# A decoder layer on one core: dense quarters taken by the slab, gated sums turned a step later, a reciprocal moved

## The chip, the cores and the metric

The kernel runs on one core of a Trainium2 chip. The time is the device time of one execution, in microseconds (us). The core has four compute engines with queues of their own: TensorE (PE in the rows; PEld is its weight load), VectorE (DVE), ScalarE (ACT) and GpSimd (POOL). SyncE (SP) issues the large weight loads. Engines wait for each other through semaphores.

## The reference, cut to what matters

One decoder layer, 256 tokens, width 2048, all in float32.

```python
mod = silu(c) @ w_ada + b_ada                       # six vectors: shift, scale, gate, twice
h = rmsnorm(x) * (1 + sc_a) + sh_a
mixed = sigmoid(g_a) * (out_a @ w_proj_a) + sigmoid(g_b) * (hm @ w_proj_b)   # attention, mLSTM
x = x + gt_a * (mixed @ w_out)
t = rmsnorm(x) * (1 + sc_m) + sh_m
# router: one of 4 groups, then 2 of its 8 experts for each token, softmax weights -> comb
hg, hu = t @ w_gate_e, t @ w_up_e                   # 32 experts, each 2048 x 512
out = sum over experts of (silu(hg) * hu * comb) @ w_down_e                  # each 512 x 2048
x = x + gt_m * out
```

An expert's weights are 12 MB: 8 slabs of 1 MB for gate and up, 4 for down.

## The kernel before, in words

The first half of the program is the mixer: projections of the normed input (`half_pair`, `wide_gemm`), attention and mLSTM, all with each weight split into two float32r halves (`split`, L202 on ScalarE and L203 on VectorE). A half slab of weights is pushed, split, and multiplied one push later; after each push `tick` runs one step of the generators that wait in the list `side` and, now and then, one product of the adaLN matrix (`ada`, L156, on VectorE).

The mixer's end: `gate(i)` and `proj(i)` (L900 on) run over column blocks of 512. For blocks 4 to 7, `proj` multiplies the product by the gate (L905), adds the other mixer's part (L907), and calls `turn_over`, which transposes the sum with eight PE transposes (tile `mt`) and splits it into `mxh` and `mxl`. Then the output projection (`wo`) runs over 16 blocks of 128 columns; beside it `scaled` and `logit` (L1018 on) build the scaled residual `xg`, the router's logits `lb` and the shift's part `sh`. Expert 0 is a static dense expert: its 12 slabs are loaded during the output projection.

The router (L1066 on): the reciprocal norm as a column (`rcol`) and as a broadcast tile (`rstd2`, L1074), then group choice, expert choice and a ranking of the experts by their number of tokens, mostly tiny VectorE operations. Expert numbers reach SyncE through register loads (L1245, L1252). `tiles` turns the residual back to rows beside it.

The experts: `first` is expert 0, dense, over all 256 tokens and a shift column; a second dense one (`HEAVY`) is the expert ranked first. The others go in stacks of four (once two) experts (`LIGHT`), each with 32 (64) gathered tokens, so that four matmuls share the array. `prep` gathers a stack's tokens: masks `G` on VectorE, transposes `cb`, 64 matmuls `xb`. A light step uses one slab of each of its experts; a stack has 8 gate-up steps (tile `gu<-ring,xg`), then `silu` and the next stack's `prep`, then 4 down steps (`yb`, then `ob` back to tokens). A dense slab is used in four quarters, each four matmuls, with a `yield 0.25` after each (`gu<-xg,raw` for the first dense expert, `gu<-xg,ring` and `dd<-at,ring` for the second).

What sets the order: SyncE follows program order (`manual_schedule`). PE follows it too while `in_order` is set, which it is from the first light step until the dense stream ends; elsewhere a planner orders PE, VectorE and ScalarE. The loop at L1430 on merges the two streams: it takes the next piece from the dense stream (`i` = 0) unless that one is ahead by its share (`done[i] / total[i]`, with a dense share `HEAVY_SHARE` of 0.2; pieces of the second dense expert count twice). After an `"act"` piece the other stream is forced `SKIP[i]` times. Before the loop, `BEFORE` quarters of the first dense expert are put in the program.

Loads go through `ring` (`next_slot`, L1091 on): slots are taken from the front and put back at the end, so they serve in turn. The ring starts with four slots (three `w8`, one `v8`); `freed` adds one for each slab of the first dense expert that is used up, except slabs 0 and 7, until it has 14. A slot that is new in the ring is a fresh tile (load at L1104), which takes over the space of an earlier tile of its pool. A slot in use again is loaded at L1106. SyncE waits there until the matmuls of the slot's last slab are done, and all later loads stand behind.

Of the kernel before, what the change touches and what calls it, by code (L numbers as in the profile page):

```python
# [13 lines left out]
AF = mybir.ActivationFunctionType  # L14
# [4 lines left out]
P = 128  # L19
T = 256  # L20
D = 2048
KT = D // P
# [8 lines left out]
SKIP = [1, 2]  # L31
BIG2 = 3
FOR_XG = (0, 7)
EARLY = (1, 1)
BEFORE = 6
FIRST = "prrrtrtrtrtr"
HEAVY_SHARE = 0.2
W4 = 3
# [30 lines left out]
def decoder_layer_kernel(ctx, tc, xT, c, pos, cols_d, const_d, mask_d, w_ada, w_head, w_half, w_blk, w_mlv, w_pa, w_pb, w_out,  # L69
                         w_uq, w_ukv, w_rt, w_gu, w_dn, outT):  # L70
    nc = tc.nc
    act, vec, pool = nc.scalar, nc.vector, nc.gpsimd
# [20 lines left out]
    def bank(name):  # L93
        return psum.tile([P, 512], F32, name=name, tag="bank")
# [15 lines left out]
    def by2(x):  # L110
        return x.rearrange("p (a t) -> p a t", t=T)
# [4 lines left out]
    mod = keep.tile([P, 96], F32, name="mod")  # L116
# [3 lines left out]
    ones = keep.tile([P, P], F32, name="ones")  # L120
    rstd2 = keep.tile([P, T], F32, name="rstd2")
    warm = keep.tile([P, 1], F32, name="warm")
    rcol = keep.tile([P, 2], F32, name="rcol")
    brow = keep.tile([P, 36], F32, name="brow")
    lg = keep.tile([P, 2, 40], F32, name="lg")

    def col(name, i=0, n=1, p0=0, p1=P):
        s = COLS[name].start + i
        return cols[p0:p1, s:s + n]
# [64 lines left out]
    def pair(name, dt=F32):  # L194
        return by2(t2(name, dt))
# [12 lines left out]
    def split_act(src, name, make=None):  # L208
        hi, lo = [make(name + x, "tx" + x, F32R) if make else pair(name + x, F32R) for x in "hl"]
        act.activation(hi, src, AF.Copy)  # L210
        vec.tensor_tensor(lo, src, hi.bitcast(F32), op=ALU.subtract)
        return hi, lo
# [27 lines left out]
    side, pend = [], []  # L240
    ticks, headless = [0], [False, 0]

    def step():
        while side:
            try:
                next(side[0])
                return
            except StopIteration:
                side.pop(0)
# [546 lines left out]
    def pick(lst, i):  # L796
        return lambda k: lst[k // 2][i][:, k % 2]
# [88 lines left out]
        wide_gemm([w_blk[i, g] for g in range(4)], "ga", hhk, hlk, after)  # L886

    def turn_over(nh):
        for j in range(2):
            b = bank("mt")  # L890
            for i in range(2):
                for tt in range(2):
                    o = i * T + tt * P
                    pe.transpose(b[:, o:o + P], gated[nh][tt][:, (2 * j + i) * P:(2 * j + i + 1) * P], ident)
            mxs[2 * nh + j] = split_act(by2(b), "mx")

    def proj(i):
        nh = i % 4
        src, w = (oT, w_pa) if i < 4 else (hm, w_pb)

        def after(bs):
            store = mixed if i < 4 else gated
            for tt in range(2):
                t = store[nh][tt]
                vec.tensor_tensor(t, bs[tt], t, op=ALU.mult)  # L905
                if i >= 4:
                    vec.tensor_tensor(t, t, mixed[nh][tt], op=ALU.add)  # L907
            if i >= 4:
                turn_over(nh)

        if nh == 0:
            while src[3] is None:
                step()
        wide_gemm([w[nh, g] for g in range(2)], "pjb", pick(src, 0), pick(src, 1), after)
# [76 lines left out]
    wr = a1.tile([P, KT * 36], F32, name="wr")  # L991
    nc.scalar.dma_start(wr, w_rt)
    accs = t2("accs")
    lb, sh = bank("lb"), bank("sh")
# [20 lines left out]
    def logit(n, xg):  # L1015
        yield
        w = wr[:, n * 36:(n + 1) * 36]
        for tt in range(2):  # L1018
            pe.matmul(lb[:, tt * 36:(tt + 1) * 36], xg[:, tt * P:(tt + 1) * P], w, start=n + tt == 0, stop=False)
        for m in ((0, 1) if n == 0 else (n + 1,) if n < KT - 1 else ()):  # L1020
            pe.matmul(sh[:, 0:36], mod[:, 48 + m:49 + m].to_broadcast([P, P]), wr[:, m * 36:(m + 1) * 36], start=m == 0,
                      stop=m == KT - 1)
        if n == KT - 2:
            vec.tensor_tensor(brow, sh[:, 0:36], col("route_b", 0, 36), op=ALU.add)

    for n in range(KT):
# [23 lines left out]
    through = [0]  # L1050
# [20 lines left out]
    pe.matmul(sb2[:, :T], ones, accs[:, :T], start=True, stop=False)  # L1071
    pe.matmul(sb2[:, :T], ones, last[0][:, :T], start=False, stop=True)
    act.activation(rstd2, sb2[:, :T], AF.Sqrt, bias=epsc, scale=1.0 / D)
    vec.reciprocal(rstd2, rstd2)  # L1074
    for _ in range(EARLY[1]):
        next(first)
    phase_a.close()
# [320 lines left out]
    for _ in (*route, *tiles):  # L1398
        pass
    pinned.clear()  # L1400

    def unit(u):
        if u[0] == "dense":
            r = u[1]
            return dense(lambda: expert(r), lambda: R["perm"][:, r:r + 1].to_broadcast([32, P]), lambda: R["qT"][:, 1], xgs)
        return stack(u[1], u[2], u is LIGHT[-1])
# [18 lines left out]
    n_heavy = HEAVY_SHARE * n_light  # L1425
    for _ in range(BEFORE):
        next(first)
    pre[LIGHT[0][1]] = prep(*LIGHT[0][1:])
    in_order.append(1)
    streams, total, done = [heavy, light], (n_heavy, n_light), [0.0, 0.0]  # L1430
    forced = []
    while any(streams):
        i = forced.pop(0) if forced else int(done[0] / total[0] > done[1] / total[1])
        if not streams[i]:
            i = 1 - i
        got = next(streams[i], None)
        if got == "act":
            forced = [1 - i] * SKIP[i]
        elif got:
            done[i] += got * (2 if i == 0 and through[0] == 12 else 1)  # L1440
        else:
            streams[i] = None
        if not streams[0]:
            in_order.clear()
# [164 lines left out]
```

## Time and profile before

| What | Value |
|---|---|
| median of 3 runs (lowest to highest) | 1629.94 us (1629.08 to 1633.8) |
| the profiled execution's own time | 1629.09 us |
| its span on the profile | 1627.2 us |
| PE busy | 1382.4 us, 85% |
| VectorE busy | 750.0 us, 46% |
| ScalarE busy | 441.7 us, 27% |
| DMA moved | 560.70 MB, mean 345 GB/s |

The page gives busy time over the whole span, so it mixes stages with different limits. The slices (its second part) cut the span into 40 equal pieces and show the stages apart. The chain follows the last instruction back, at each step to what released it. A window row gives the busy time of each engine within one stretch, the granted TensorE clock (1.00 is 2.4 GHz) and the rate of the DMA.

### The profile page before, as it was taken

How to read it: one execution, taken by the hardware profiler on the slowest of the kernel's cores; microseconds unless marked ns; L12 is line 12 of the kernel's file. 1: busy time of each engine (PE TensorE's matmuls, PEld its weight loads, DVE VectorE, ACT ScalarE, POOL GpSimd, SP SyncE). 2: the span in 40 equal slices, each digit the busy share in tenths (PEclk: the TensorE clock that was granted, in tenths of full speed). 3: DMA queues.
4: the chain of work that ended last, by engine and by line, in shares of the span. 5: the costliest groups of instructions: out<-in, count | busy, mean ns of one | idle time of the engine just before them, and what ended most of it. 6: DMA issues, size and time to landing. Idle time of an engine off the chain costs nothing.

```text
span 1627.2 us, 21430 instructions
## 1 busy us (share of the span) xinstructions
PE 1382.4 (85%) x8290; PEld 960.9 (59%) x8290; DVE 750.0 (46%) x1113; ACT 441.7 (27%) x646; POOL 83.8 (5%) x91
## 2 busy tenths in 40 slices
PE   7899999999999999999978997867889756656766
PEld 5698998878877777899844753533445313213212
DVE  5878699879777778975401220210222301201202
ACT  3134765445754464333200100100100001001000
POOL 0150014000000000022000000000000000000000
PEclk9899999999999999999999997988999978888899
DMA  9978767888677788886498999899999699999997
GB/s 369 395 276 334 275 222 284 315 288 301 259 263 262 256 351 341 306 327 246 165 376 372 387 421 421 365 394 421 421 416 420 286 421 421 420 420 421 420 421 302
DMA packets 78877, 560.70 MB, mean 345 GB/s; under 512 B 8753, under 2 KB 9009, under 8 KB 12721
## 3 DMA queue, kind: packets, MB, share of 16 engines
q1 hardware_dynamic: 78482, 558.84, 86.4%
q8 instruction: 67, 1.10, 0.3%
q10 hardware_dynamic: 288, 0.44, 0.1%
q14 instruction: 40, 0.33, 0.1%
HBM read 569.73 MB, written 2.10 MB: 351 GB/s over the span
## 4 chain that ended last, share of the span: by engine, by line
PE 45%; DMA 33%; DVE 10%; issue 5%; ACT 3%; SPq 1%; POOL 0%; ACTq 0%; DVEq 0%; POOLq 0%
DMA ring<-in_w_gu_dram 24%; DMA ring<-in_w_dn_dram 8%; PE gu L78 7%; PE hp L78 6%; PE wo L78 5%; PE ga L78 5%; DVE raw L156 4%; PE pjb L78 3%; PE yb L78 3%; DVE whl L203 3%; PE dd L78 2%; PE xb L78 2%; PE vb L78 2%; PE hb L78 2%; SPq L1106 1%
## 5 line engine op out<-in xcount | busy, mean ns | idle before, releaser
L78 PE MATMUL gu<-ring,xg 128*32 128x512 f32 (+1 forms) x1664 | 259.1, 721 | 132.2 <-DMA ring<-in_w_gu_dram 132.1
L203 DVE TENSOR_TENSOR whl<-raw,whl 128x1024 fp32r<-128x1024 f32 (+1 forms) x210 | 253.2, 1216 | 82.0 <-ACT whl L202 81.1
L202 ACT ACTIVATE whl<-raw 128x1024 fp32r<-128x1024 f32 (+1 forms) x210 | 216.9, 1037 | 256.4 <-PE ga L78 61.4
L78 PEld LDWEIGHTS gu<-ring,xg 128*32 128x32 f32 (+1 forms) x1664 | 64.0, 130 | 305.8 <-DMA ring<-in_w_gu_dram 157.4
L156 DVE SCALAR_TENSOR_TENSOR raw<-raw,cond 128x2048 f32<-128x2048 f32 x96 | 220.7, 2300 | 16.5 <-DMA raw<-in_w_ada_dram 16.4
L78 PE MATMUL ga<-whl,hh 128*128 128x512 f32 x512 | 169.5, 401 | 1.3 <-DVE whl L203 1.3
L78 PE MATMUL yb<-ring,aT 128*32 128x512 f32 (+1 forms) x832 | 117.4, 655 | 56.5 <-DMA ring<-in_w_dn_dram 52.8
L78 PE MATMUL hp<-hh,whl 128*128 128x256 f32 x640 | 120.9, 288 | 3.4 <-DVE whl L203 3.2
L1332 DVE SCALAR_TENSOR_TENSOR s<-gu,wc,s 128x512 f32<-128x512 f32 x7 | 5.2, 750 | 231.2 <-PE gu L78 231.2
L78 PEld LDWEIGHTS ga<-whl,hh 128*128 128x128 f32 x512 | 96.0, 188 | 25.4 <-issue 3.1
L1259 DVE SCALAR_TENSOR_TENSOR xs<-ob,mod,xs 128x256 f32<-128x256 f32 x112 | 46.5, 477 | 136.4 <-PE ob L78 136.4
L1331 ACT ACTIVATE s<-gu 128x512 f32<-128x512 f32 x7 | 4.2, 596 | 384.2 <-PE gu L78 384.2
L78 PEld LDWEIGHTS yb<-ring,aT 128*32 128x32 f32 (+1 forms) x832 | 30.7, 120 | 127.0 <-issue 92.1
L78 PEld LDWEIGHTS hp<-hh,whl 128*128 128x128 f32 x640 | 101.9, 194 | 5.8 <-DVE whl L203 4.2
L78 PE MATMUL ga<-whl,hl 128*128 128x512 f32 x256 | 99.9, 390 | 0.0
L78 PE MATMUL wo<-mxh,whl 128*128 128x256 f32 x512 | 96.8, 286 | 0.2 <-DVE whl L203 0.2
L78 PE MATMUL hp<-hl,whl 128*128 128x256 f32 x320 | 91.2, 285 | 0.0
L78 PEld LDWEIGHTS wo<-mxh,whl 128*128 128x128 f32 x512 | 80.9, 191 | 0.4 <-DVE whl L203 0.4
L78 PE MATMUL wo<-mxl,whl 128*128 128x256 f32 x256 | 72.4, 283 | 0.0
L1344 ACT ACTIVATE yh<-yb 128x512 fp32r<-128x512 f32 (+1 forms) x29 | 16.9, 583 | 199.2 <-PE yb L78 198.7
L1279 DVE TENSOR_REDUCE wc<-cb 128x1 f32<-128x256 f32 x7 | 3.0, 424 | 137.9 <-PE cb L83 137.9
L78 PEld LDWEIGHTS hp<-hl,whl 128*128 128x128 f32 x320 | 62.1, 194 | 0.6 <-issue 0.5
(370 smaller groups left out, 2014.7 us busy)
## 6 DMA issues: line engine op xcount, KB each, us to landing
ring<-in_w_gu_dram SPq DMA_DIRECT2D x216, 1024.0 KB, 15.5
ring<-in_w_dn_dram SPq DMA_DIRECT2D x104, 1024.0 KB, 18.8
raw<-in_w_ada_dram SPq DMA_DIRECT2D x96, 1024.0 KB, 6.8
raw<-in_w_blk_dram SPq DMA_DIRECT2D x32, 1024.0 KB, 6.2
raw<-in_w_half_dram SPq DMA_DIRECT2D x20, 1024.0 KB, 5.0
raw<-in_w_out_dram SPq DMA_DIRECT2D x16, 1024.0 KB, 5.1
raw<-in_w_head_dram SPq DMA_DIRECT2D x16, 704.0 KB, 7.2
raw<-in_w_mlv_dram SPq DMA_DIRECT2D x8, 1024.0 KB, 4.8
```

The costliest lines, as they stand in the source:

```text
L78: ins = nc.tensor.matmul(*args, **kw)
L156: vec.scalar_tensor_tensor(raw, raw, 1.0, cond, op0=ALU.mult, op1=ALU.mult, accum_out=mod[:, i:i + 1])
L202: keep(act.activation(hi, raw, AF.Copy))
L203: keep(vec.tensor_tensor(lo, raw, hi.bitcast(F32), op=ALU.subtract))
L1106: nc.sync.dma_start(slot[:, s], src[:, s], cond=cond())
L1259: vec.scalar_tensor_tensor(xs[:, d], src, mod[:, 80 + d:81 + d], xs[:, d], op0=ALU.mult, op1=ALU.add)
L1279: vec.tensor_reduce(wc, cb[:, :T], axis=AX.X, op=ALU.add)
L1331: act.activation(s, gu[0], AF.Silu)
L1332: vec.scalar_tensor_tensor(s, gu[1], wc, s, op0=ALU.mult, op1=ALU.mult)
L1344: act.activation(yh[:, s], yb[:, s], AF.Copy)
```

## The change

The stream takes a whole slab (four quarters) of the second dense expert at once, and after a light stack's `"act"` the dense stream is forced once instead of twice while that expert runs. Two quarters fewer of the first dense expert are put ahead of the streams. `turn_over` becomes a generator in `side`: for the first three column blocks its transposes come one step after the sums, and its two halves come in two steps. In the router the shift's products use a one-column operand and give one row; ScalarE copies the row, and one matmul with ones spreads it over the partitions. The reciprocal of `rstd2` moves from the router's start to behind the router and the row tiles, kept in program order there.

```diff
--- before.py
+++ after.py
@@ -32,7 +32,7 @@
 BIG2 = 3
 FOR_XG = (0, 7)
 EARLY = (1, 1)
-BEFORE = 6
+BEFORE = 4
 FIRST = "prrrtrtrtrtr"
 HEAVY_SHARE = 0.2
 W4 = 3
@@ -886,6 +886,8 @@
         wide_gemm([w_blk[i, g] for g in range(4)], "ga", hhk, hlk, after)
 
     def turn_over(nh):
+        if nh < 3:
+            yield
         for j in range(2):
             b = bank("mt")
             for i in range(2):
@@ -893,6 +895,7 @@
                     o = i * T + tt * P
                     pe.transpose(b[:, o:o + P], gated[nh][tt][:, (2 * j + i) * P:(2 * j + i + 1) * P], ident)
             mxs[2 * nh + j] = split_act(by2(b), "mx")
+            yield
 
     def proj(i):
         nh = i % 4
@@ -906,7 +909,7 @@
                 if i >= 4:
                     vec.tensor_tensor(t, t, mixed[nh][tt], op=ALU.add)
             if i >= 4:
-                turn_over(nh)
+                side.append(turn_over(nh))
 
         if nh == 0:
             while src[3] is None:
@@ -1018,9 +1021,10 @@
         for tt in range(2):
             pe.matmul(lb[:, tt * 36:(tt + 1) * 36], xg[:, tt * P:(tt + 1) * P], w, start=n + tt == 0, stop=False)
         for m in ((0, 1) if n == 0 else (n + 1,) if n < KT - 1 else ()):
-            pe.matmul(sh[:, 0:36], mod[:, 48 + m:49 + m].to_broadcast([P, P]), wr[:, m * 36:(m + 1) * 36], start=m == 0,
-                      stop=m == KT - 1)
+            pe.matmul(sh[0:1, 0:36], mod[:, 48 + m:49 + m], wr[:, m * 36:(m + 1) * 36], start=m == 0, stop=m == KT - 1)
         if n == KT - 2:
+            act.activation(brow[0:1], sh[0:1, 0:36], AF.Copy)
+            pe.matmul(sh[:, 0:36], ones[0:1], brow[0:1], start=True, stop=True)
             vec.tensor_tensor(brow, sh[:, 0:36], col("route_b", 0, 36), op=ALU.add)
 
     for n in range(KT):
@@ -1071,7 +1075,6 @@
     pe.matmul(sb2[:, :T], ones, accs[:, :T], start=True, stop=False)
     pe.matmul(sb2[:, :T], ones, last[0][:, :T], start=False, stop=True)
     act.activation(rstd2, sb2[:, :T], AF.Sqrt, bias=epsc, scale=1.0 / D)
-    vec.reciprocal(rstd2, rstd2)
     for _ in range(EARLY[1]):
         next(first)
     phase_a.close()
@@ -1398,6 +1401,7 @@
     for _ in (*route, *tiles):
         pass
     pinned.clear()
+    tc.keep_in_program_order(vec.reciprocal(rstd2, rstd2))
 
     def unit(u):
         if u[0] == "dense":
@@ -1433,9 +1437,12 @@
         i = forced.pop(0) if forced else int(done[0] / total[0] > done[1] / total[1])
         if not streams[i]:
             i = 1 - i
+        whole = i == 0 and through[0] == 12
         got = next(streams[i], None)
+        if whole and got not in (None, "act"):
+            got += sum(next(streams[0]) for _ in range(3))
         if got == "act":
-            forced = [1 - i] * SKIP[i]
+            forced = [1 - i] * (1 if through[0] == 12 else SKIP[i])
         elif got:
             done[i] += got * (2 if i == 0 and through[0] == 12 else 1)
         else:
```

## Rows read from the trace of the kernel before

**Rows 1.** the page's slices (40 of 40.7 us each): GB/s that the DMA moved in each

```profile
GB/s 369 395 276 334 275 222 284 315 288 301 259 263 262 256 351 341 306 327 246 165 376 372 387 421 421 365 394 421 421 416 420 286 421 421 420 420 421 420 421 302
```

**Rows 2.** windows: from:to length, busy us (xcount) of each engine, clock, DMA share, GB/s

```profile
1050.00:1060.00 10.00, 8.16 (x57) 5.03 (x56) 3.85 (x10) 2.30 (x8) 0.00 (x0) 1.00 0.37 126
...
1280.00:1290.00 10.00, 9.96 (x69) 5.04 (x66) 4.43 (x10) 0.60 (x1) 0.00 (x0) 1.00 0.06 26
...
1290.00:1300.00 10.00, 1.89 (x8) 1.33 (x8) 2.94 (x10) 0.00 (x0) 0.00 (x0) 0.83 0.70 274
```

**Rows 3.** the chain that ended last, expert stretch: start us, us, engine, tile, line

```profile
1056.80 1.75 PE gu L78 x8
...
1058.56 0.33 SPq L1106
...
1166.80 7.15 PE xb L78 x64
...
1289.96 1.94 PE dd L78 x8
...
1291.92 0.34 SPq L1106
```

**Rows 4.** one tile's view, ring, 780 to 1310: time from issue to landing

```profile
DMA to landing us min/median/max: 4.8/13.9/20.8
```

**Rows 5.** PE's timeline, light gate-up step 1: start us, us, operation, [idle before]

```profile
819.40 4.95 PE L78 MATMUL gu<-ring,xg 128*32 128x512 f32 x32 [5.69 <-DMA ring<-in_w_gu_dram]
```

**Rows 6.** PE's timeline, light step 7, gather's transposes, down step 0

```profile
883.91 3.64 PE L78 MATMUL gu<-ring,xg 128*32 128x512 f32 x32 [0.97 <-DMA ring<-in_w_gu_dram]
...
893.05 0.30 PE L83 MATMUL cb<-const,G 128*128 128x128 f32 x1 [2.95 <-DVE G L1271]
...
909.68 3.64 PE L78 MATMUL yb<-ring,aT 128*32 128x512 f32 x32 [0.69 <-ACT aT L1338]
```

**Rows 7.** windows, end of the first dense expert

```profile
880.00:890.00 10.00, 9.03 (x56) 4.90 (x54) 1.40 (x4) 0.69 (x4) 0.00 (x0) 1.00 0.55 217
...
910.00:920.00 10.00, 10.00 (x72) 5.73 (x68) 2.43 (x5) 0.60 (x1) 0.00 (x0) 1.00 0.73 278
```

**Rows 8.** SyncE's timeline, the same stretch

```profile
887.62 0.33 SPq L1104 DMA_DIRECT2D ring<-in_w_dn_dram  x1
```

**Rows 9.** PE's timeline, first transposes of three column blocks

```profile
624.37 0.44 PE L83 MATMUL mt<-const,gx 128*128 128x128 f32 x2 [1.38 <-DVE gx L907]
...
638.70 0.41 PE L83 MATMUL mt<-const,gx 128*128 128x128 f32 x2 [2.07 <-DVE gx L907]
...
652.33 0.44 PE L83 MATMUL mt<-const,gx 128*128 128x128 f32 x2 [1.41 <-DVE gx L907]
```

**Rows 10.** windows: end of the projections, output projection

```profile
650.00:667.00 17.00, 14.11 (x69) 11.08 (x69) 17.00 (x21) 6.38 (x7) 0.00 (x0) 1.00 0.75 276
...
667.00:775.00 108.00, 106.71 (x884) 105.59 (x882) 74.78 (x85) 38.64 (x49) 21.11 (x26) 1.00 0.76 288
```

**Rows 11.** the chain, output projection and router

```profile
705.38 1.07 ACT whl L202
...
741.32 0.22 PE sh L78 x2
...
783.66 0.20 PE ob L78 x4
```

**Rows 12.** one tile's view, rstd: xcount, ns min/median/max, first and last start

```profile
L1074 DVE RECIPROCAL rstd<-rstd x1: 1754/1754/1754, 776.3 to 776.3; 128x256 f32<-128x256 f32 x1
```

**Rows 13.** windows: second dense expert, its last third, light stacks alone

```profile
951.00:1292.00 341.00, 281.56 (x1693) 147.94 (x1692) 60.54 (x150) 24.97 (x55) 0.00 (x0) 0.92 0.96 396
...
1160.00:1292.00 132.00, 123.96 (x730) 68.67 (x722) 39.87 (x95) 14.73 (x32) 0.00 (x0) 0.99 0.93 382
...
1300.00:1380.00 80.00, 49.81 (x326) 17.69 (x326) 5.48 (x12) 5.34 (x11) 0.00 (x0) 0.79 1.01 421
```

## The prediction

> **What bounds the kernel now.** I read the page's slices first, then ten-microsecond windows, then the chain, and only then single instructions. The slices show two regimes [rows 1]. In the first half the DMA rate lies mostly between 222 and 395 GB/s and TensorE (PE) is nearly always busy. From the 20th slice on the experts run, and from the 24th on the rate sits at 416 to 421 GB/s in most slices: there the kernel waits for weights. One slab is 1 MB, so at 421 GB/s it takes 2.49 us, and whatever keeps the DMA below 421 in that half is paid in full, because nothing later makes it up. The windows name the two worst holes [rows 2]: 126 GB/s from 1050 to 1060, 26 and 274 GB/s from 1280 to 1300. Lost transfer time: (421-126)/421 x 10 = 7.0 us; (421-26)/421 x 10 = 9.4 and (421-274)/421 x 10 = 3.5, together 12.9 us. Sum 19.9 us.
>
> The chain shows who holds the DMA up [rows 3]. At 1056.80 PE takes one quarter of a dense gate-up slab, and only at its end does SyncE issue the next load (1058.56), with the queue empty by then. At 1291.92 it is the same with a quarter of a dense down slab.
>
> Why: the ring has 14 slots, handed out in program order. A slab's slot is wanted again 14 loads later, and SyncE issues in order, so one late slot holds all loads. A dense slab is used in four quarters, and the stream puts light steps (four loads each) between them. I counted, along the stream's rule, how many loads that PE does not need yet are under way when a dense slab's last quarter ends. For the second dense expert's twelve slabs before: 5 for eight of them, 7 and 9 for two, and 1 for two: gate-up slab 3 (its last quarter stands behind down slabs 0 to 2 of the stack at rank 7, and its slot is the one that down slab 3's first load wants) and down slab 3 (its last quarter stands behind the stack at rank 1 and the next stack's first gate-up step). With one load ahead the DMA runs dry, since a load into an idle queue takes at least 4.8 us to land [rows 4]. These two are the holes, in place and releaser.
>
> **Part 1: four quarters at once.** The same count with the new rule gives 13 for all twelve slabs. 13 loads are 32 us of transfer; a refill needs 4.8 us. To use up the difference, PE would have to be 27 us behind. The heaviest pile after a landing that the new order makes is a stack step (3.64 us [rows 6]), the next stack's gather (7.15), a whole slab (7.0, four quarters of 1.75 [rows 3]) and a down step (3.64): 21 us, of which four or five loads' landing (10 to 12 us) lies beside. So both holes should close: -19.9 us. No PE work is added; the new rule changes order only. Behind a whole slab a light step waits up to 5.3 us more on PE than behind one quarter; its loads are in SBUF by then, and SyncE has other free slots. The forced count after a light stack drops from two quarters to one slab, which the same count includes.
>
> **Part 2: the first dense expert starts two quarters later (BEFORE 4).** The light stack's gather and first step move ahead of two quarters, 3.6 us earlier; in exchange the ring holds four slots instead of five when step 1 is loaded, so all its loads wait for step 0. In the old trace PE then waits 5.69 us for that step [rows 5]. Walking the loads by hand at 2.49 us each and 4.8 us for the first, step 1 comes 1 to 2 us earlier, step 3 1 us later, and by step 7 (883.91 before) [rows 6] both orders meet, since from about 840 on the DMA is the limit in both. Value 0; bounds -3.6 (all of the earlier start kept) and +4 (one and a half slabs lost).
>
> The end of that expert changes more. The DMA falls to 217 and 278 GB/s at 880 and 910 [rows 7]: 4.8 and 3.4 us. The first is the load at 887.62 [rows 8]: a new ring tile that takes over the first stack's gathered input, so it waits for gate-up step 7 (ends 887.55) and is the second load behind it. In the new order that tile is the sixth load behind it. The second is PE late with down step 0 (909.68), after VectorE held the gather's transposes up (a wait of 2.95 us before the first of them) [rows 6]; now the gather comes ahead of the dense expert's VectorE work. Bounds 0 (VectorE still late, the hole moves) and -8.2; I take -5.0, the first hole and little of the second.
>
> **Part 3: turning one step later.** PE idles 1.38, 2.07 and 1.41 us before the transposes of the first three column blocks, because four VectorE operations stand between the last projection matmul and them [rows 9]: 4.9 us at most. With a half slab of matmuls in between that wait is covered, but VectorE is then next: from 650 to 667 it is busy 17.00 of 17 us [rows 10]. What it can gain is idle time it has earlier, so I take -1.5; bounds 0 and -4.9. The fourth block keeps its first wait; its second half moves into the output projection, where PE has 1.3 us idle in 108 [rows 10], at a bound of +2.1, a wait like the longest of the three.
>
> **Part 4: the router.** In the output projection PE time is on the path. The shift products with a broadcast 128-column operand take 0.22 us a pair; the nearest ones with a one-column operand take 0.10 (four matmuls in 0.20) [rows 11]. Sixteen pairs: 16 x 0.12 = 1.9 us; at least 0, if other weight loads fill the time. Added are one ScalarE copy and a broadcast matmul that waits for it; output-projection matmuls queue behind that one on PE, and the next VectorE multiply of the residual behind those. With a few matmuls put ahead of it this costs +0.2; directly behind its copy, and that behind a copy of weights (1.07 us [rows 11]), about +1.3. Sum -1.7, bounds -1.9 and +1.3. The broadcast reciprocal, 1754 ns [rows 12], leaves the chain in front of the expert choice, so the first loads go out 1.7 us earlier; but it lands in front of the gather's VectorE work, which is what PE waits for after part 2. Value 0, inside the bounds of part 2.
>
> **Sum** against the profiled execution's 1629.09 us (span 1627.2 and 1.9 around it): -19.9 - 5.0 - 1.5 - 1.7 = -28.1, so 1601.0. The median of the runs lies 0.85 above the profiled execution: 1602.
>
> **Rivals.** (a) PE becomes the bound where the second hole was. From 1160 to 1292 it is busy 123.96 of 132 us [rows 13], so at most 8.0 of the 12.9 us come back: 1607. For it: that stretch holds two gathers and four dense slabs. Against: before 1160 PE has idle time to run ahead in (281.56 busy of 341 from 951 to 1292 [rows 13]). (b) The shallow ring at the start costs three slabs, 7.5 us, kept to the end: 1609. For it: the DMA is far from 421 there. Against: the meeting point at step 7. (c) The change does not free slots earlier, because the matmul that frees a slot is not the last of its own slab but one queued later: holes and part 2's gain stay, 1629.9 - 3.2 = 1627. Against: both late loads go out within 0.1 us of the end of the quarter that the count names [rows 3]. (d) Slower: the PE clock. In 1300 to 1380 PE waits for loads, is busy 49.81 of 80 us, and the granted clock averages 0.79, a mix of 1.2 and 2.4 GHz [rows 13]. Whole slabs bunch PE's work and leave longer waits; if dense slabs then ran at 1.2 GHz, each would take 14 instead of 7 us, 84 us for twelve. PE's 281.56 would become 366 in a stretch of 341: +25 us, less parts 2 to 4, 1646. It decides from 6 slow slabs on that PE is the bound (39 us idle after the holes close, 7 each), and from 9 on that the kernel is slower. Against: in 1160 to 1292 the clock is 0.99, and a slab's start is after a light step that has already run.
> The Trainium skill, page "TensorE: Matmul & The Clock Gate", section "HAM oscillation — how this bites in real kernels", states this rule: bursts of matmuls between DMA waits fall back to the slow clock each time. By that rule case (d) holds and the sum would be its 1646; the trace agrees that the clock falls in such waits, but not in the stretch where the dense slabs are thick.
>
> **How the numbers follow.** Chances: forecast 0.60, (a) 0.20, (b) 0.11, (c) 0.05, (d) 0.04. About 0.3% (4.9 us) is what a measurement of this kernel can tell from no change. Forecast, (a) and (b) are faster: 0.91; (c) is within 0.3%: 0.05; (d) slower: 0.04. The range: from 1602 down by the open ends of parts 2 to 4 (3.6, 3.2, 3.4 and 0.2: 10), up over (a) and (b) with some of both: 1592 to 1616.
>
> **What would show it.** Part 1: no window of the second dense expert below 400 GB/s, and SyncE never waiting for a single dense quarter. Part 2: step 7 of the first stack within 3 us of its place relative to the router, and no 217 GB/s window behind it. Part 3: the three idle times before transposes gone, the output projection starting 1 to 2 us earlier. Part 4: sixteen short pairs, and the expert choice 1.7 us nearer to the last logits. Wrong would be a new wait of SyncE on a whole slab, or a clock near half in dense slabs.

## The result, and the profile after

The changed kernel takes 1612.32 us (median of four runs, 1609.77 to 1617.16); the kernel before, on the same chip, 1629.70 (1629.08 to 1633.80). The ratio is 0.9892, with a 95% interval of 0.9863 to 0.9920: faster by 1.1%, 10 us above the forecast of 1602, inside the range. The profiled execution is the slowest of the four (span 1615.3 us), so I compare stages and not spans.

The page's slices after, GB/s of 40 pieces of 40.4 us, answer [rows 1]:

```profile
GB/s 348 391 298 323 289 205 286 316 305 286 268 262 265 263 313 351 329 330 235 156 263 398 408 422 420 420 420 420 421 421 421 421 420 420 421 421 421 421 420 269
```

From the 24th slice on nothing is below 420 but the last. The windows after that answer [rows 2] and [rows 7] (from:to length, busy us of PE, weight load, VectorE, ScalarE, GpSimd, clock, DMA share, GB/s):

```profile
880.00:890.00 10.00, 9.12 (x64) 5.42 (x56) 0.00 (x0) 0.00 (x0) 0.00 (x0) 1.00 1.01 422
...
910.00:920.00 10.00, 9.31 (x76) 5.91 (x75) 5.33 (x15) 4.18 (x9) 0.00 (x0) 1.00 0.96 398
...
1040.00:1060.00 20.00, 15.15 (x109) 7.77 (x111) 2.95 (x6) 2.48 (x7) 0.00 (x0) 0.90 1.01 421
...
1160.00:1280.00 120.00, 111.18 (x656) 63.63 (x650) 34.32 (x84) 13.56 (x27) 0.00 (x0) 0.96 1.01 420
1280.00:1300.00 20.00, 14.53 (x96) 5.23 (x94) 6.82 (x19) 0.60 (x1) 0.00 (x0) 0.91 1.01 419
```

Both holes and both dips are gone. So the gain came from where I said, and something else took a part of it. Where, shows when one looks at when each stage begins and ends. The views of the tiles `pjb` (projections), `wo` (output projection) and `order` (expert choice) give the first and last start of each group; first before, then after:

```profile
L78 PE MATMUL pjb<-whl,oTh x128: 387/389/799, 470.5 to 611.4; 128*128 128x512 f32 x128
L78 PE MATMUL pjb<-whl,hmh x128: 388/394/484, 611.7 to 664.2; 128*128 128x512 f32 x128
...
L78 PE MATMUL wo<-mxh,whl x512: 276/283/469, 666.2 to 772.4; 128*128 128x256 f32 x171
...
L1177 DVE CAST order<-ob x1: 215/215/215, 783.9 to 783.9; 1x64 int32<-1x64 f32 x1
```

```profile
L78 PE MATMUL pjb<-whl,oTh x128: 387/389/799, 472.3 to 613.2; 128*128 128x512 f32 x128
L78 PE MATMUL pjb<-whl,hmh x128: 388/396/478, 613.4 to 660.5; 128*128 128x512 f32 x128
...
L78 PE MATMUL wo<-mxh,whl x512: 278/283/582, 662.4 to 779.2; 128*128 128x256 f32 x171
...
L1180 DVE CAST order<-ob x1: 215/215/215, 788.5 to 788.5; 1x64 int32<-1x64 f32 x1
```

The table has these stages for every kernel run here, in us of its profiled execution: A from the start to the first `pjb`, B first to last `pjb`, C from there to the last `wo`, D to `order`, E to the first light step, F from there to the end; then B to F summed. A is the same instructions in all of them and took 467.3 to 473.3, so B to F tells more than the span. B also moves without an edit: where `turn_over` is at once it took 192.1 with a granted clock of 1.00 and 193.7 with 0.99, where it is late 186.6 with 1.00 and 188.3 (188.6 in e7) with 0.99. Each ratio is to runs of the kernel before on the same chip, whose medians went from 1626.50 to 1629.81, so medians of four runs, on different chips above all, cannot rank kernels that lie 3 us apart.

| kernel | A | B | C | D | E | F | B to F | median (ratio to before, interval) |
|---|---|---|---|---|---|---|---|---|
| before | 470.5 | 193.7 | 108.2 | 11.5 | 20.8 | 822.5 | 1156.8 | 1629.70 |
| after | 472.3 | 188.3 | 118.7 | 9.3 | 19.5 | 807.4 | 1143.0 | 1612.32 (0.9892, 0.9863 to 0.9920) |
| e1_before6 | 473.3 | 186.7 | 117.9 | 9.3 | 22.9 | 807.0 | 1143.7 | 1615.88 (0.9905, 0.9879 to 0.9931) |
| e2_wide_shift | 468.8 | 186.6 | 118.0 | 9.3 | 19.5 | 805.5 | 1138.8 | 1611.92 (0.9892, 0.9866 to 0.9917) |
| e3_turn_at_once | 470.5 | 192.1 | 109.4 | 9.3 | 19.5 | 806.2 | 1136.5 | 1609.70 (0.9872, 0.9842 to 0.9901) |
| e4_stream_only | 467.4 | 192.1 | 108.3 | 11.5 | 20.8 | 805.5 | 1138.1 | 1609.15 (0.9874, 0.9850 to 0.9898) |
| e5_two_quarters | 470.6 | 193.7 | 108.3 | 11.5 | 20.8 | 812.9 | 1147.1 | 1616.97 (0.9918, 0.9891 to 0.9946) |
| e6_warm_two_later | 469.3 | 186.6 | 114.9 | 9.3 | 19.5 | 806.8 | 1137.0 | 1609.20 (0.9876, 0.9848 to 0.9904) |
| e7_warm_one_later | 467.3 | 188.6 | 117.6 | 9.7 | 19.9 | 810.5 | 1146.4 | 1614.12 (0.9904, 0.9879 to 0.9929) |
| e8_no_router_part | 470.5 | 186.6 | 115.6 | 11.5 | 17.3 | 806.3 | 1137.3 | 1607.08 (0.9861, 0.9836 to 0.9886) |
| e9_splits_in_order | 471.1 | 186.6 | 114.5 | 9.3 | 19.9 | 804.9 | 1135.3 | 1608.45 (0.9876, 0.9852 to 0.9899) |
| e10_best | 470.8 | 186.7 | 114.6 | 11.2 | 18.2 | 806.0 | 1136.6 | 1611.80 (0.9899, 0.9867 to 0.9931) |
| e11_stream_and_four | 468.6 | 193.7 | 108.2 | 11.5 | 17.3 | 806.4 | 1137.0 | 1607.20 (0.9860, 0.9838 to 0.9882) |
| e12_moved_warm_again | 469.6 | 186.6 | 115.6 | 11.5 | 17.3 | 807.0 | 1138.0 | 1609.02 (0.9867, 0.9846 to 0.9887) |

From before to after: B -5.4, C +10.5, D -2.2, E -1.3, F -15.1, together -13.8 before rounding. The forecast had -1.5 in B, -1.7 in C and D, -24.9 in F. Two stages are off by about 10 us each: the output projection (C) and the experts (F).

**Inside F.** I went over F in windows of 5 us from the first light step to 35 us before the last weights land, and added up (421 - rate) / 421 x 5, the transfer time lost; the last column is what moved in the 40 us before the last weights land.

| kernel | first 70 us | 70 to 130 us | later | all | MB in the last 40 us |
|---|---|---|---|---|---|
| before | 9.8 | 8.1 | 22.0 | 39.9 | 15.9 |
| after | 17.2 | 1.0 | 0.8 | 19.0 | 14.6 |
| e1_before6 | 12.2 | 7.4 | 1.0 | 20.6 | 14.4 |
| e4_stream_only | 11.0 | 7.1 | 1.2 | 19.2 | 14.5 |
| e5_two_quarters | 12.2 | 7.3 | 10.6 | 30.0 | 16.0 |
| e11_stream_and_four | 16.0 | 1.0 | 0.8 | 17.8 | 14.4 |

The holes are worth 21 us and the end of the first dense expert 7, a little more than forecast. The first 70 us lose 7.4 us more than before. PE's timeline, light step 0 before, then light steps 0, 1, 7 and down step 0 after, against [rows 5, 6]:

```profile
804.67 3.64 PE L78 MATMUL gu<-ring,xg 128*32 128x512 f32 x32
```

```profile
807.92 3.64 PE L78 MATMUL gu<-ring,xg 128*32 128x512 f32 x32
...
824.90 6.43 PE L78 MATMUL gu<-ring,xg 128*32 128x512 f32 x32 [7.93 <-DMA ring<-in_w_gu_dram]
...
897.34 3.64 PE L78 MATMUL gu<-ring,xg 128*32 128x512 f32 x32 [1.54 <-DMA ring<-in_w_gu_dram]
...
915.64 1.93 PE L78 MATMUL yb<-ring,aT 128*32 128x512 f32 x16 [0.69 <-ACT aT L1341]
```

From step 0 to step 7 it takes 89.4 us; before it took 79.2. From there to down step 0, 18.3 instead of 25.8. SyncE's timeline shows why the start is slower; first before, then after (L1104 and L1107: a slot new in the ring; L1106 and L1109: a slot in use again):

```profile
813.74 0.33 SPq L1104 DMA_DIRECT2D ring<-in_w_gu_dram  x1
824.37 13.54 SPq L1106 DMA_DIRECT2D ring<-in_w_gu_dram  x8
```

```profile
816.52 0.38 SPq L1107 DMA_DIRECT2D ring<-in_w_gu_dram  x1
831.35 2.60 SPq L1109 DMA_DIRECT2D ring<-in_w_gu_dram  x4
```

With four slots all loads of a step wait for the step before: after, SyncE issues nothing from 816.5 to 831.4, 14.8 us; before it was 10.6, and then eight loads could go out instead of four.

### The profile page after: what moved, and what is told of

Same layout as the page of the kernel before. It is cut to its first block, busy times and chain, and to the rows that moved or that the text cites. A ratio compares the mean times of both kernels' runs of the same rounds, so it can differ in the third digit from the quotient of the medians.

```text
span 1615.3 us, 21544 instructions
## 1 busy us (share of the span) xinstructions
PE 1385.6 (86%) x8292; PEld 964.4 (60%) x8292; DVE 747.5 (46%) x1113; ACT 441.1 (27%) x647; POOL 87.7 (5%) x91
## 4 chain that ended last, share of the span: by engine, by line
PE 47%; DMA 36%; DVE 9%; issue 5%; ACT 3%; SPq 0%; POOL 0%; ACTq 0%; DVEq 0%; POOLq 0%
DMA ring<-in_w_gu_dram 23%; DMA ring<-in_w_dn_dram 11%; PE gu L78 7%; PE hp L78 6%; PE wo L78 6%; PE ga L78 5%; PE pjb L78 5%; PE yb L78 3%; DVE raw L156 3%; PE dd L78 3%; DVE whl L203 3%; PE hb L78 2%; PE vb L78 2%; PE xb L78 2%; DMA raw<-in_w_ada_dram 2%
## 5 line engine op out<-in xcount | busy, mean ns | idle before, releaser
L156 DVE SCALAR_TENSOR_TENSOR raw<-raw,cond 128x2048 f32<-128x2048 f32 x96 | 220.1, 2294 | 17.4 <-DMA raw<-in_w_ada_dram 8.9
L78 PE MATMUL yb<-ring,aT 128*32 128x512 f32 (+1 forms) x832 | 123.1, 687 | 52.3 <-DMA ring<-in_w_dn_dram 48.7
L78 PE MATMUL wo<-mxh,whl 128*128 128x256 f32 x512 | 101.0, 294 | 3.7 <-ACT whl L202 2.4
```

The costliest lines, as they stand in the source:

```text
L78: ins = nc.tensor.matmul(*args, **kw)
L156: vec.scalar_tensor_tensor(raw, raw, 1.0, cond, op0=ALU.mult, op1=ALU.mult, accum_out=mod[:, i:i + 1])
```

## The experiments

**The stream rule alone.** e4 is the kernel before with the last hunk of the diff and nothing else.

```diff
+        whole = i == 0 and through[0] == 12
         got = next(streams[i], None)
+        if whole and got not in (None, "act"):
+            got += sum(next(streams[0]) for _ in range(3))
         if got == "act":
-            forced = [1 - i] * SKIP[i]
+            forced = [1 - i] * (1 if through[0] == 12 else SKIP[i])
```

> The kernel before with only the stream's rule changed (second dense expert by the whole slab, one forced piece after a light stack). Theory (a dense slab held over light steps is what emptied the queue): no window of the second dense expert under 400 GB/s, everything up to the first light step as before, and 18 to 20 us gained: 1609 to 1612. Rival (PE becomes the bound from 1160 on): 8 to 15 us gained, 1615 to 1622, with SyncE waiting on PE in that stretch.

1609.15 us, ratio 0.9874, and F falls by 17.0; no 10 us window from 930 to 1560 is below 415 GB/s. The theory held and the rival fell. So this hunk carries the whole gain. The other three parts together add nothing to it: their medians cannot be told apart, and by the stages B to F they lose 4.9 us (1138.1 to 1143.0).

**Half of it.** e5 takes two quarters at a time (`got += next(streams[0])`), to see whether the count of loads ahead is what closes a hole.

> The kernel before with the stream taking two quarters (not four) of the second dense expert at a time, and one forced dense piece after a light stack's act. My count of loads that are ahead of PE when a dense slab's last quarter ends: 5 for seven slabs, 7 for one, 9 for four, and 1 for none (before: 1 for two, the two holes). Theory (the hole is a matter of the loads ahead, and 5 were enough for eight slabs of the kernel before): both holes close, no window between 950 and 1580 under 400 GB/s, 1608 to 1612 us, like the run with the stream rule alone (1609.2). Rival (the hole goes by how long a slab is held, which is about halved): both holes stay at about half of their 20 us, 1617 to 1622 us.

1616.97 us, between the two forecasts. The windows of e5 at both places:

```profile
1040.00:1060.00 20.00, 18.50 (x139) 9.12 (x137) 4.72 (x11) 3.07 (x8) 0.00 (x0) 1.00 0.99 405
1260.00:1270.00 10.00, 9.25 (x47) 3.57 (x46) 1.92 (x5) 1.79 (x3) 0.00 (x0) 1.00 1.01 422
1270.00:1280.00 10.00, 10.00 (x53) 5.18 (x50) 5.05 (x13) 1.19 (x2) 0.00 (x0) 1.00 0.58 237
1280.00:1290.00 10.00, 6.64 (x50) 3.55 (x48) 4.99 (x15) 0.00 (x0) 0.00 (x0) 1.00 0.67 265
```

The first hole closes, as the count says; the second stays at (421-237)/421 x 10 + (421-265)/421 x 10 = 8.1 of 12.9 us. PE's and SyncE's timelines of e5 there:

```profile
1260.97 7.09 PE L78 MATMUL yb<-ring,aT 128*64 128x512 f32 x32 [0.75 <-ACT aT L1338]
...
1269.13 3.65 PE L78 MATMUL yb<-ring,aT 128*64 128x512 f32 x16
...
1273.87 3.65 PE L78 MATMUL yb<-ring,aT 128*64 128x512 f32 x16
...
1278.51 3.62 PE L78 MATMUL dd<-at,ring 128*128 128x256 f32 x16
```

```profile
1282.16 11.04 SPq L1106 DMA_DIRECT2D ring<-in_w_gu_dram  x11
```

The load that wants the slot of down slab 3 goes out at 1282.16, as the slab's last two quarters end, and ten more follow in the next 11 us; before it none had gone out since 1258. Ahead of those quarters PE works off four down steps of the stack of two experts, without a pause from 1260.97 on. A step of that stack has two loads, 5 us of transfer, for about 4.7 us of PE; a step of a stack of four has four loads, 10 us, for about the same. Five loads ahead cover 12.5 us; here PE needs 21 before it frees the slot. So the theory holds for the first hole and falls for the second: loads ahead have to be set against the PE time in front of the freeing quarter, and only 13 were enough at both places. The rival came near in time, since half of the 22.0 us lost remains (10.6 in the table), but not in its mechanism, for it had both holes halved. e4 and e5 both force one dense piece after a light stack; no run has that alone, so its own share is not shown.

**The late turning.** e3 is the changed kernel with `turn_over` called at once, as before.

```diff
-                side.append(turn_over(nh))
+                turn_over(nh)
```

> The changed kernel with the transposes of the gated sums right behind the sums, as before the change; all else as changed. Theory (the later turning gained 5 us in the projections, but with it the planner put the pinned square-root warm-up of ScalarE ahead of the weight splits of output block 13, and PE starved there): PE's three waits before the transposes are back (about 5 us), the output projection takes 105 to 108 us instead of 116.8, and the time is 1605 to 1609. Rival (the later turning is a plain gain, the output projection is long for another reason): 1616 to 1618.

C falls from 118.7 to 109.4 and B rises by 3.8: 5.5 gained in all, 2.6 by the medians, whose intervals overlap. PE's waits before the transposes are back (4.9 us in three), and the first to last `wo` matmul takes 107.3 us, as the theory said; the rival fell. By the stages, late turning loses more in the output projection than it gains in the projections. How, show PE's and ScalarE's timelines of the changed kernel:

```profile
750.04 0.64 PE L78 MATMUL lb<-wr,xg 128*128 128x36 f32 x4 [0.97 <-DVE xg L1014]
752.62 0.58 PE L78 MATMUL wo<-mxh,whl 128*128 128x256 f32 x1 [1.95 <-ACT whl L202]
753.00 0.41 PE L78 MATMUL wo<-mxl,whl 128*128 128x256 f32 x1
753.88 0.79 PE L78 MATMUL wo<-mxh,whl 128*128 128x256 f32 x2 [0.47 <-DVE whl L203]
```

```profile
749.69 0.42 ACT L1036 ACTIVATE sq<-xs 128x256 f32<-128x256 f32 x1 [5.78 <-DVE xs L1034]
750.13 1.28 ACT L1042 ACT_TABLE_LOAD   x1
751.42 0.20 ACT L1042 ACTIVATE warm<-epsc 128x1 f32<-128x1 f32 x1
751.53 1.99 ACT L202 ACTIVATE whl<-raw 128x1024 fp32r<-128x1024 f32 x2
```

ScalarE stood idle for 5.78 us, waiting to square output block 12, and both weight splits of block 13 were queued behind that square, the function table and the warm-up. In e3 the last split ahead of the same square (750.53 there) is this one, so both splits of block 13 were done when the square came:

```profile
746.42 1.06 ACT L202 ACTIVATE whl<-raw 128x1024 fp32r<-128x1024 f32 x1 [0.99 <-PE wo L78]
```

In the changed kernel PE ran out of split weights and its granted clock fell. Windows after, then of e3:

```profile
750.00:760.00 10.00, 7.55 (x39) 7.14 (x40) 4.75 (x5) 3.49 (x5) 0.72 (x1) 0.66 0.55 213
760.00:770.00 10.00, 7.85 (x50) 7.33 (x49) 4.33 (x5) 3.71 (x5) 0.73 (x1) 0.83 0.67 260
```

```profile
745.00:755.00 10.00, 9.95 (x83) 9.43 (x82) 5.96 (x7) 3.39 (x5) 2.80 (x4) 1.00 0.82 296
755.00:765.00 10.00, 8.87 (x73) 8.28 (x72) 4.95 (x6) 4.40 (x6) 1.40 (x1) 1.00 0.71 279
```

Over all of C PE idles 7.7 us after and 2.8 before (sum of the waits in its timeline), and the clock costs, as an estimate, 10 x 0.34 + 10 x 0.17 = 5.1: with the 4.9 of waits more that is 10.0 of the 10.5 that C lost. The number of its matmuls has not changed (but for the two that spread the shift's row); the planner put ScalarE's work in another order. Three kernels change that order.

```diff
e6, e7:
-            if n == KT - 4:
+            if n == KT - 2:          # e7: KT - 3
                 tc.keep_in_program_order(act.activation(warm, epsc, AF.Sqrt))
e9:
     for n in range(KT):
+        if n == 0:
+            pinned.append(1)         # split() keeps program order
         b = bank("wo")
...
     flush()
+    pinned.clear()
```

> The changed kernel with the ScalarE warm-up of the square root, which is kept in program order, put two output blocks later, behind all weight splits of the output projection. Theory (with the late turning, ScalarE has the square of block 12, the function-table load and the warm-up ahead of the splits of block 13, PE runs out of split weights at about 752 to 765 and the clock falls): first to last wo matmul takes 106 to 109 us instead of 116.8, so 1604 to 1608 us. Rival (ScalarE or VectorE is behind for want of time since the late turning, and the warm-up's place does not matter): still 114 to 117 us, 1611 to 1614 us.

> The same with the warm-up one output block later: the splits of block 13 come ahead of it, four splits of the last blocks stay behind it. Theory: most of the gain of the run with two blocks, 1604 to 1609 us; the first to last wo matmul takes 106 to 110 us. Rival (it only moves the stall to the next block's splits): 1611 to 1614 us.

> The changed kernel with the weight splits of the output projection (ScalarE copy, VectorE difference) kept in program order, so that the first split of a block stands ahead of the square of the block before it, not both splits behind it; the warm-up stays where it was. Theory (after the late turning the planner put both splits of blocks 13 to 15 behind the square of the block before, which waits for TensorE, so TensorE waits 2 to 3 us a block for split weights and its clock falls): first to last wo matmul 106 to 109 us instead of 116.8, no PE wait for whl over 1 us, granted clock 1.00, 1603 to 1606 us. Rival (the late turning leaves VectorE or the DMA behind in this stretch, and the order of the splits only shows it): 112 to 117 us, 1609 to 1613 us.

C is 114.9, 117.6 and 114.5 us. With the warm-up two blocks later it improves by 3.8, with one block hardly: the stall goes to the next splits. e6 still has both splits of a block behind a square, with PE waits of 0.97, 0.43 and 0.76 at 745 and at 755. With the splits pinned the waits for ScalarE shrink to 0.80 and 0.45 us, but PE now waits 1.28 us at 687 for VectorE's half of a split, which is queued behind an adaLN product (`raw<-raw,cond`, 2.29 us). So the place of the warm-up and the order of the splits are some 4 us of the 9; neither theory's number was met. Of the other 5, PE's waits are 3.7 (6.5 us in e6 and in e9, 2.8 before), and the granted clock of 0.99 is about one more. Some of these waits are for splits, others for VectorE's `xg` (0.97 twice in e6) and sums `gx` (2.16 in e9); I found no single cause for them, and that stays open. What makes e7 also slower in F (810.5) I did not find out.

**Two quarters fewer ahead.** e1 is the changed kernel with `BEFORE = 6`; e11 is e4 with `BEFORE = 4`.

> The changed kernel with six instead of four quarters of the first dense expert put ahead of the streams; all else as changed. Theory (the shallow ring at the start cost about 10 us): the stretch from the first light step 0 to step 7 goes from 89.4 us back to 79 to 81 (it was 79.2 before the change), SyncE finds a fifth slot for step 1, and the time falls by 5 to 9 us, to 1603 to 1607. Rival (the weights are the limit there in both orders, so what is late at step 7 is made up behind it, in the hole that the new order closes): the stretch shortens, but the time stays within 2 us of 1612.

> The kernel before with the stream rule and two quarters fewer ahead of the streams; no late turning, no router part. Theory (of the changed kernel's four parts these two gain, 17 to 20 us and 3 us; the late turning and the router's part together lose 3 to 5 us): 1604 to 1607 us, 2 to 4 us below the run with the stream rule alone. Rival (two quarters fewer only helped in the changed kernel, where the late reciprocal delayed the first gather): 1608 to 1611 us.

e1 is not faster than the changed kernel but, by its median, 3.6 us slower, with overlapping intervals: the theory that `BEFORE` 4 costs the missing time fell. From step 0 to step 7 it does take 81.5 us instead of 89.4. The first 70 us do lose 5 us less with 6 (12.2 against 17.2), but the end of the first dense expert loses 6.4 more. The window of e1 there is the dip of [rows 7] again:

```profile
890.00:900.00 10.00, 6.85 (x46) 2.89 (x44) 3.74 (x10) 1.56 (x6) 0.00 (x0) 1.00 0.58 221
```

F is the same within 0.4 us (807.0 and 807.4), and what is left are the two quarters themselves in front of the first light step: 22.9 against 19.5 us in E. From e4 to e11 the same shows: E 20.8 to 17.3, F +0.9. The medians, 1609.15 to 1607.20, go the way of that theory, but come from two chips, and the intervals overlap.

**The router's part.** e2 is the changed kernel with the broadcast shift products; e8 has the other three parts, the warm-up moved as in e6, and no router part; e12 is e8 again beside e11; e10 is e8 with the splits pinned instead of the warm-up moved.

```diff
e2 (to the changed kernel):
-            pe.matmul(sh[0:1, 0:36], mod[:, 48 + m:49 + m], wr[...], start=m == 0, stop=m == KT - 1)
+            pe.matmul(sh[:, 0:36], mod[:, 48 + m:49 + m].to_broadcast([P, P]), wr[...], start=m == 0, stop=m == KT - 1)
```

> The changed kernel with the router's shift products as they were before (128-column broadcast operand, no copy of the row on ScalarE, no spreading matmul). Theory (this part is worth its 1.7 us and has nothing to do with the 10.6 us that the output projection became longer): 1612 to 1615, and the output projection from its first to its last matmul stays 116 to 118 us. Rival (the new ScalarE copy and the matmul that waits for it brought the loss): the output projection falls to about 107 us and the time to 1602 to 1606.

> The kernel before with the stream rule, two quarters fewer ahead, the late turning, and the warm-up two output blocks later; the router's part (narrow shift products, late reciprocal) is left out. Theory (the router's part is worth nothing: the run with the wide products was 0.4 us below the changed kernel, and the late reciprocal only moves first-dense-expert matmuls from before the expert choice to behind it): within 1.5 us of the run with the warm-up two blocks later and the router's part. Rival (the router's part is worth its 1.7 us, hidden by the stall so far): 1.5 to 2.5 us slower than that run.

> The same kernel as the run without the router's part (stream rule, two quarters fewer, late turning with the warm-up two output blocks later), beside the run above on the same chip. Theory (what the late turning gains in the projections, 5.5 us, the output projection gives back, 5 to 6 us, even with the warm-up moved): within 2 us of the run above. Rival (late turning with the warm-up moved is worth 2 us or more): 2 to 4 us below the run above.

> The kernel before with the stream rule, two quarters fewer ahead, the late turning, and the output projection's splits kept in program order; no router part, the warm-up at its old place. Theory (the parts add up once the planner's order is out of the way: 5.5 us of the late turning, 3 us of the two quarters, 17 us of the stream rule): 1602 to 1605 us. Rival (as above): 1606 to 1609 us, like the run without the router's part.

The narrow products gain nothing: e2 1611.92 to 1612.32. C stays long in e2 (118.0), so the copy of the row and the matmul that spreads it did not bring the loss there; the rival fell. PE's timeline, a logit group, its shift pair and the next `wo`, in e11 (broadcast) and in e3 (one column):

```profile
706.53 0.64 PE L78 MATMUL lb<-wr,xg 128*128 128x36 f32 x4 [0.32 <-DVE xg L1011]
707.00 0.39 PE L78 MATMUL sh<-wr,mod 128*128 128x36 f32 x2
707.22 0.36 PE L78 MATMUL wo<-mxh,whl 128*128 128x256 f32 x1
```

```profile
707.17 0.64 PE L78 MATMUL lb<-wr,xg 128*128 128x36 f32 x4 [0.32 <-DVE xg L1011]
707.74 0.23 PE L78 MATMUL sh<-wr,mod 128*1 128x36 f32 x2
707.90 0.39 PE L78 MATMUL wo<-mxh,whl 128*128 128x256 f32 x1
```

The narrow pair itself takes 0.16 us to the next `wo` instead of 0.22, but it starts 0.57 after the group instead of 0.47, so the whole is 0.73 against 0.69. The logit group there waits for `xg`; in the groups that do not wait the whole is 0.61 or 0.62 against 0.58 or 0.59, and where the pair stands behind a `wo` matmul it takes 0.36 or 0.37 from that one's start to the next `wo`, against 0.26. Only the first group, with two pairs, is shorter (0.76 against 0.88). C is 109.4 in e3 and 108.2 in e11: +1.2. The reciprocal shortens D by 2.2 and lengthens E by the same (e11 has 17.3, e3 with the same `BEFORE` 19.5): matmuls of the first dense expert that PE did in the router's waits are now done behind them. From the last `wo` to the first light step PE is busy in all but 0.3 us, in e3 and in e11, so there is nothing to gain by moving work:

```profile
772.00:800.80 28.80, 28.49 (x209) 25.18 (x209) 17.77 (x79) 9.84 (x22) 0.00 (x0) 1.00 0.39 147
```

```profile
770.40:799.20 28.80, 28.46 (x208) 25.20 (x207) 18.00 (x79) 9.84 (x22) 0.00 (x0) 1.00 0.39 147
```

e8 against e6, 1607.08 to 1609.20, points the same way, 2.1 us below where the theory had at most 1.5, but the intervals overlap. e12 and e11 are 1.8 us apart, on one chip: what late turning gains in B (7.1) it gives back in C (7.4), as that theory said. Of the 7.1, 1.6 are the clock: from 630 to 640 e11 has a granted clock of 0.83, and at an equal clock B falls by 5.5 (192.1 to 186.6). e10's name was too hopeful: its median, 1611.80, meets neither forecast, and by stages it is near e9 (1136.6 and 1135.3), though two of its four runs took 1614.

The lowest medians, 1607.1 to 1607.2, are those of e8 and e11, 5 us under the changed kernel; their intervals overlap with its own. e11 is the plainest: the stream rule and two quarters fewer ahead.

## Why the prediction was right, and where it was wrong

**Part 1** was right in cause, place and transfer time: 21.2 us (22.0 to 0.8) against 19.9. Rival (a), PE as the new bound, and rival (c), slots freed no earlier, fell: 420 GB/s from 1160 to 1280, with PE busy 111.18 of 120. Rival (d) fell too: the clock there is 0.96, and the matmuls of the dense slabs take 377, 380 and 484 ns (least, median, most), in the kernel before as after:

```profile
L78 PE MATMUL gu<-xg,ring x256: 377/380/484, 969.5 to 1159.3; 128*128 128x257 f32 x128
```

But F shrank by 17.0 in e4, where 20.7 us of transfer time came back. By F, the step that failed is "whatever keeps the DMA below 421 in that half is paid in full". F is one execution of each kernel, and by the medians e4 gained 20.7 us, so these 3.7 us are not certain. The last 10 us before the last weights land, before, in e5 (holes not all closed), and after:

```profile
1604.82:1614.82 10.00, 8.56 (x63) 2.82 (x60) 3.83 (x9) 0.60 (x1) 0.00 (x0) 1.00 0.82 325
```

```profile
1595.00:1605.00 10.00, 7.99 (x60) 2.73 (x58) 3.13 (x7) 0.60 (x1) 0.00 (x0) 1.00 0.86 343
```

```profile
1592.89:1602.89 10.00, 10.00 (x72) 3.88 (x72) 4.51 (x10) 1.20 (x2) 0.00 (x0) 1.00 0.59 225
```

The loads land at the same times before the last one, but without the holes 1.3 to 1.5 MB had already moved earlier, 3.1 to 3.6 us at 421 GB/s, in each of the four kernels of the table that have none. That some of the 16 DMA engines finish last while others are already idle would explain it (their mean busy share is 0.59 at the end); the trace does not show it engine by engine.

**Part 2** had the right two places, and one term wrong. The end of the first dense expert gave 7.1 us (8.1 to 1.0; I took 5.0, bound 8.2). At the start I took 0 with the step "by step 7 both orders meet": they do not; step 7 comes 10.2 us later after step 0 than before. I had seen that all loads of step 1 wait for step 0, but took the DMA to be the limit in both orders from about 840 on; after, it moves 372 and 373 GB/s from 840 to 880, because with four slots each step's loads wait for one step. Against e1, which differs in `BEFORE` alone, the start costs 5.0 us of transfer time, beyond my bound of 4, and one slab (2.5 us: 234.9 MB instead of 236.0 have moved when the first light step begins) is left for later; the end of the first dense expert gives back 6.4. That is rival (b)'s mechanism, but it is not "kept to the end". What saves the part is the term I had as a bound: the first light step comes 3.5 us earlier, and that is kept. Together -2.4 us (5.0 + 2.5 - 6.4 - 3.5), for a forecast of -5.0.

**Part 3** was wrong in sign. The three idle times are gone, as the first transposes of the second column block after show, with no wait before them:

```profile
639.42 0.60 PE L83 MATMUL mt<-const,gx 128*128 128x128 f32 x4
```

B gained 5.4 to 5.5 at an equal clock, more than the 4.9 that I had as the most; the step "VectorE is then next" was too strict for B. But the only cost that I gave the output projection was one wait of 2.1 us; it was 9.3 (118.7 to 109.4). What I did not cost is that this stage is ordered by the planner from its own estimates: changing what precedes it changes ScalarE's and VectorE's order in it, and PE, which had 1.3 idle us in 108 [rows 10], has no slack for that.

**Part 4**: the pair's price came from four matmuls of another shape, `ob` [rows 11], of which only the first pair follows a matmul with a 128-column operand; measured, the pair with its start is 0.03 to 0.04 us dearer behind the logits and 0.11 behind `wo`, not 0.12 cheaper. The reciprocal's value of 0 was right, but not by the reason given: it does land among the gather's VectorE work, yet PE does not wait for it, since PE is full there (28.49 of 28.80 us above).

The sum, term by term, forecast to measured in the profile: F -24.9 to -15.1 (holes -21.2, end of the first dense expert -7.1, start +7.4, the slab left for later +2.5, the last 40 us +3.1: -15.3); E, no term, to -1.3 (-3.5 and +2.2); B and C for late turning -1.5 to +3.9; the router's part -1.7 to -1.0 (C +1.2, D -2.2). That is -28.1 to -13.5, where the table says -13.8; by medians the change was -17.4. Of the 14.6 us between the two sums 9.8 lie in F: the start, where I had taken 0, cost 9.9 with the slab left for later, and the last 40 us 3.1, while the holes and the end of the first dense expert gave 3.4 more than forecast. Late turning, which I costed only where it acts, missed by 5.4, the router's part by 0.7, and E gave 1.3 that I had not counted. The time lies in that part of the range which I had opened for rivals (a) and (b); neither held as stated, so that it fell inside is in part luck.

The Trainium skill, page "TensorE: Matmul & The Clock Gate", section "HAM oscillation — how this bites in real kernels", which stood beside rival (d), tells of bursts of matmuls between DMA waits that start again at the slow clock each time. The dense slabs do not show it: their matmuls are as long after as before. In the output projection the clock did fall, to 0.66 from 750 to 760, but beside waits of 0.97, 1.95 and 0.47 us for VectorE and ScalarE, not for the DMA.

## What to carry to other kernels

A hole in a transfer-bound stretch can be priced from the windows and its cause counted from the order of slots; but set the loads ahead against the PE time in front of the freeing instruction. Here the stage got back 3.7 us less than the windows said, in one execution of each kernel. A stage whose engine is 99% busy and whose order a planner makes is not neutral ground: an edit just ahead of it needs a price for that stage too, and a run with that edit undone. Price a small matmul from one that follows the same neighbour, not from one of the same size elsewhere.

## What the hardware showed that I had not expected

- Without holes after the 24th slice, the DMA's busy share in the last 10 us is 0.55 to 0.59 in after and e4; with a hole at 1270 to 1300 (before, e5) it is 0.82 to 0.86, at the same spacing of the last landings. That some of the 16 engines run ahead in a long full stretch, and that a hole lets the others catch up, would explain it; the trace does not name the engine of a packet, so this is argued, not shown.
- After waits of 0.97, 1.95 and 0.47 us (for VectorE's `xg` and for two weight splits) in an otherwise full stretch the granted clock was 0.66 over 10 us, a mix of 1.2 and 2.4 GHz (0.50 from 754 to 758, 1.00 from 760 to 762): matmuls of 128x256 followed each other at 0.64 us for three (755.33 to 755.97) instead of 0.36 (759.40 to 759.76).
- Going from a 128-column operand to a one-column operand costs PE 0.09 to 0.10 us (0.57 against 0.47 from the logit group's start to the pair, 0.21 against 0.12 from a `wo` matmul's start), more than the pair itself saves (0.06 behind the logits, nothing behind `wo`).
